# Modulation products of a two-layer diffusion backbone: in pairs on TensorE, one more sixth summed on VectorE, and a norm's first high parts on VectorE

## The chip, the cores and the metric

The kernel runs on one core of a Trainium2 chip. The metric is the device time of one execution in microseconds (us); the comparison is between medians of several executions of the kernel before and of the changed kernel.

## The reference, cut to what matters

Two layers of a hybrid diffusion backbone act on 256 latent tokens and 256 context tokens of width 1024. A conditioning vector gives, for each layer, a modulation of six parts (shift, scale and gate for the mixer and for the feed-forward part), for the latent and the context stream:

```python
mod = jax.nn.silu(c) @ w_mod[l] + b_mod[l]
mod_c = jax.nn.silu(c_ctx) @ w_mod[l] + b_mod[l]
sh1, sc1, g1, sh2, sc2, g2 = jnp.split(mod[:, None, :], 6, axis=-1)
h = rmsnorm(x, g_pre_mix[l]) * (1 + sc1) + sh1
y, y_ctx = token_mixer(h, hc, lp, row, col, ctx_out)
x = x + g1 * rmsnorm(y, g_post_mix[l])
h2 = rmsnorm(x, g_pre_ffn[l]) * (1 + sc2) + sh2
x = x + g2 * rmsnorm(conv_ffn(h2, ...), g_post_ffn[l])
```

The mixer has four branches (latent attention, a bidirectional mLSTM, window attention, a Fourier mix), each gated by a product of `h` with a 1024x1024 matrix and summed. The reference is in float32.

## The kernel before, in words

Activations stand feature by feature: eight tiles of 128 features by the tokens. Each float32 factor of a large product is split into a high and a low part, and each product is three matmuls: high by high (line L236), and the two cross terms (L237, L238). The weights come by DMA on SyncE's queue into `st`; ScalarE casts the high part `wh` (L216), VectorE subtracts it to get the low part `wl` (L217).

The order of TensorE's instructions is written out by hand: wherever a stage would leave TensorE waiting for another engine, `fill(us)` takes matmuls from independent work of another stage (most of them gate products of `merge`). VectorE's, ScalarE's and GpSimd's orders are made by the scheduler, save inside `in_order()`. Each engine's instructions stand in a fixed order once the program is built.

The modulation is done by `mod_rounds` (L608 to L671). A round is one of the six parts: eight k tiles of `w_mod`, each [128, 4x256], which arrive by DMA (L625) on GpSimd's queue in the first layer (rounds 2 to 4) and on SyncE's elsewhere. A step is one k tile: four 32-column matmuls of line L653, whose records come in eights. `between(n)` takes n steps from `queue`, and `fill` takes them where they are fillers. A round that is listed in `vector` is summed on VectorE instead: two sums over the k tiles, one for each stream, by L640 for the first tile and L642 for the other seven, and at the end eight matmuls with a column of ones (L648, 16 records). A round ends with a transpose `kr` (L656) and an addition of the bias (L664, L667). In the first layer round 3 was summed on VectorE; rounds 2 and 4 were taken by `pause` (L896), `mla` (L960) and by the merge, one step at a time.

The places of the first layer that the steps speak of: the latent attention's softmax (`nbias` L831, exponential on ScalarE L835, reciprocal L840, scaled `pp` L841, transposed on TensorE at L847); the mLSTM's gates in `mlstm_gates` (`gcum` L1055, `gb` L1056, a product on TensorE at L1059, its copy `t` L1061, three running scans L1066 to L1068, and eight small products on TensorE at L1072); and the last head's normalisation in `mlstm` (`mden` L1216, `mab`, `mrec`, sums into `u` at L1226, then a product on TensorE at L806).

In the last layer's `channel` the norm ahead of the feed-forward part is written in order: the mean square's transposed root `rs` (L457), then for each feature tile m the product with `rs` (`t`, L405), the scaled high part `hh` on ScalarE (L408), the same number in float32 on VectorE for the first two tiles (L410) and on ScalarE for the rest (L412), and the low part `hl` by subtraction on VectorE (L414). TensorE's first products of the feed-forward part read `hh` (L236) and `hl` (L237).

Of the kernel before, what the change touches and what calls it, by code (L numbers as in the profile page):

```python
# [14 lines left out]
AF = mybir.ActivationFunctionType  # L15
ALU = mybir.AluOpType
# [6 lines left out]
T = CTX + SEQ  # L23
# [134 lines left out]
class Net:  # L158
# [237 lines left out]
        for _ in self.modulate_steps(h, m, segs, r, Am, Bm, vector):  # L396
            pass

    def modulate_steps(self, h, m, segs, r, Am, Bm, vector=False):

        nc = self.nc
        oc = self.span(segs)
        hi, lo = h[m]
        t = self.t2([T])
        nc.vector.tensor_tensor(t[:, oc], self.xcols(m, oc), r[:, oc], op=ALU.mult)  # L405
        for cs, b in segs:
            a, s = Am[:, m, b:b + 1], Bm[:, m, b:b + 1]
            nc.scalar.activation(hi[:, cs], t[:, cs], AF.Identity, scale=a, bias=s)  # L408
            if vector:
                nc.vector.tensor_scalar(t[:, cs], t[:, cs], a, s, op0=ALU.mult, op1=ALU.add)  # L410
            else:
                nc.scalar.activation(t[:, cs], t[:, cs], AF.Identity, scale=a, bias=s)  # L412
        yield
        nc.vector.tensor_tensor(lo[:, oc], t[:, oc], hi.bitcast(F32)[:, oc], op=ALU.subtract)  # L414
# [193 lines left out]
    def mod_rounds(self, l, rounds, queue, vector=(), parts=1):  # L608

        nc = self.nc
        if rounds[0] == 0:
            self.mods[l] = self.cp.tile([128, 48, 2], F32, tag=f"mod{l}", name=f"mod{l}")
        mods = self.mods[l]
        todo = [(r, q, k) for r in rounds for q in range(parts) for k in range(0, KT, parts)]
        loaded = []
        n = 256 // parts

        def load():  # L620
            if todo:
                r, q, k = todo.pop(0)
                st = self.u([parts, 4, n])
                src = self.A["wmod"][l, r, k] if parts == 1 else self.A["wmod0"][r, q, k // 2]
                queue.dma_start(out=st.rearrange("p a g n -> p (a g n)"), in_=src)  # L625
                for i in range(parts):
                    loaded.append((r, q, k + i, st[:, i]))

        def steps():
            b = self.vec[l][:, V_BMOD:V_BMOD + 48].unsqueeze(2).to_broadcast([128, 48, 2])  # L630
            while loaded or todo:
                if not loaded:
                    load()
                r, q, k, st = loaded.pop(0)
                if r in vector:
                    if k == 0:
                        sums = [self.u([4, 256]) for _ in range(2 if l < L - 1 or r < 2 else 1)]
                    for i, t in enumerate(sums):
                        if k == 0:
                            nc.vector.tensor_scalar(t, st, self.cs[:, k, i:i + 1], None, op0=ALU.mult)  # L640
                        else:
                            nc.vector.scalar_tensor_tensor(t, st, self.cs[:, k, i:i + 1], t, op0=ALU.mult, op1=ALU.add)  # L642
                    if k == KT - 1:
                        yield 1
                        ps = self.pa([256])
                        for i, t in enumerate(sums):
                            for g in range(4):
                                nc.tensor.matmul(ps[32 * g:32 * g + 32], self.col[:, i], t[:, g], start=i == 0, stop=i == len(sums) - 1)  # L648
                else:
                    if k == 0:  # L650
                        ps = self.pa([n])
                    for g in range(4):
                        nc.tensor.matmul(ps[32 * g:32 * g + 32], self.cs[:, k], st[:, g], start=k == 0, stop=k == KT - 1)  # L653
                if k == KT - 1:
                    tr = self.t2([n], tag="kr")
                    nc.vector.transpose(tr, ps)  # L656
                    src = tr.rearrange("p (t c) -> p t c", c=32)[:, :, 0:2]
                    if r < 2:
                        a = 2 // parts
                        src = src.rearrange("p (a s m) t -> p a s m t", a=a, s=2)  # L660
                        for i in range(2):
                            o = slice(8 * i + 4 * r + 2 * q, 8 * i + 4 * r + 2 * q + 2 * a)
                            fold = lambda t: t.rearrange("p (a m) t -> p a m t", a=a)
                            nc.vector.tensor_tensor(fold(mods[:, o]), src[:, :, i], fold(b[:, o]), op=ALU.add)  # L664
                    else:
                        o = slice(8 * r, 8 * r + 8)
                        nc.vector.tensor_tensor(mods[:, o], src, b[:, o], op=ALU.add)  # L667
                if k % parts == parts - 1:
                    load()
                yield 1200  # L670

        return steps(), load

# [219 lines left out]

    def pause(self, i, c0):
        self.fill(1.5 + i)
        self.between(((4, 0), (0, 5))[c0 > 0][i])  # L896

    def mla(self, l, h, c0):

        nc = self.nc  # L900
# [56 lines left out]
            self.rows = rows  # L957
            self.rope(q[rows, CTX:], ps[rows, CTX:], self.kc(C_MCOS, 256, rows), self.kc(C_MSIN, 256, rows), perm)
        self.fill(1)
        self.between((2, 3)[c0 > 0])  # L960
        rs = [slice(0, 96), slice(0, 128)]
        y = self.newy()
        room = (1.2, 1.2)
# [547 lines left out]
    def run(self):  # L1511
        nc = self.nc
# [9 lines left out]
        h = self.new_h()  # L1522
        A = None
        self.wtm = []
        mod, load = self.mod_rounds(0, (0, 1), nc.sync, parts=2)
# [3 lines left out]
        for q in range(4):  # L1529
# [6 lines left out]
            A, B = self.gain(0, 1, V_GPRE, True, "A1", ms, A), self.shift(0, 0)  # L1536
# [2 lines left out]
            if q == 0:  # L1539
                self.tm_start(h, NT)  # L1540
        self.start2()
        mod, load = self.mod_rounds(0, (2, 3, 4), nc.gpsimd, (3,))
        self.queue = [mod]
        for l in range(L):
            last = l == L - 1
            c0 = CTX if last else 0
# [16 lines left out]
    def channel(self, l, al, c0, load):  # L1563
# [11 lines left out]
        for seg in segs:  # L1575
            open_steps = []
            with self.in_order() if last else nullcontext():
                if last:
                    self.post_end([seg], True, [lambda f=f, m=m: f(m, [seg]) for m in range(2) for f in (self.scale, self.add)])
                    self.fill(1.5)  # L1580
                for m in range(KT):
                    if seg is not segs[-1] and m == 4:
                        self.post_end(segs[1:], True)
                    if m >= (2 if last else 4) or not last and seg is segs[-1]:
                        self.residual(m, [seg])
                    open_steps.append(self.modulate_steps(h, m, [seg], self.rx, A, B, last and m < 2))
                    next(open_steps[-1])
                    while len(open_steps) > (1 if last and m < KT - 1 else 0):
                        next(open_steps.pop(0), None)
                    if seg is segs[-1] and not last:  # L1590
                        self.spill(m, c0, c0)
        next(self.ws)
# [48 lines left out]
```

## Time and profile before

| what | value |
|---|---|
| median of 3 runs | 1441.56 us (1439.45 to 1442.52) |
| profiled execution | 1440.69 us |
| its span | 1438.5 us |
| mean granted TensorE clock | 0.989 |
| busy share of the span, PE / DVE / ACT / POOL | 97% / 66% / 46% / 2% |
| chain that ended last, by engine | PE 77%, DVE 7%, ACT 1%, DMA 1% |

PE is TensorE's matmuls, PEld its weight loads, DVE VectorE, ACT ScalarE, POOL GpSimd, SP SyncE. The span is that of the profiled execution, which is one run of its own; 2.2 us of its time lie outside the span. An engine's busy share is a mean over stages that have different limits, so the rows further down are taken stage by stage.

### The profile page before, as it was taken

To read this page: it belongs to the slowest core of one execution; us is meant where nothing else is said; L and a number is where in the kernel's file an instruction comes from. 1 tells how busy PE (TensorE), PEld (TensorE's weight loads), DVE (VectorE), ACT (ScalarE), POOL (GpSimd) and SP (SyncE) were. 2 spreads that over 40 slices of the span, in tenths; PEclk is the share of its full clock that TensorE was granted. 3 is DMA by queue.
4 is the path that set the end of the run, shared out by engine and by line. 5 is a ranking of instruction groups with operands and counts; after the bars stand their busy time and mean duration, and the time that the engine had idled before them with its cause. 6 is when DMAs were issued, how large, how long until landed. Compare 5 with 4: busy or idle time off the path is not lost.

```text
span 1438.5 us, 21680 instructions
## 1 busy us (share of the span) xinstructions
PE 1389.9 (97%) x8413; PEld 1165.3 (81%) x8413; DVE 949.4 (66%) x1942; ACT 659.5 (46%) x1144; POOL 33.3 (2%) x65
## 2 busy tenths in 40 slices
PE   6999999999999999999999999899999999899997
PEld 4977777777778888878888888687989898799996
DVE  5458686646644788743554658958676877766666
ACT  3446444224432655333322336656453655455553
POOL 0000000100000000000000000100000000000000
PEclk9999999999999999999999999999999999899999
DMA  9523233452122634443335432653333457255663
GB/s 373 209 71 103 89 118 103 147 163 87 59 74 88 219 125 172 172 133 103 130 115 180 160 93 79 222 199 103 106 115 118 135 189 248 85 180 176 186 184 114
DMA packets 57446, 205.86 MB, mean 143 GB/s; under 512 B 6528, under 2 KB 6912, under 8 KB 57216
## 3 DMA queue, kind: packets, MB, share of 16 engines
q1 hardware_dynamic: 50400, 179.32, 37.9%
q0 software_dynamic: 6944, 25.17, 5.1%
q8 instruction: 66, 1.08, 0.3%
q14 instruction: 36, 0.29, 0.1%
HBM read 200.27 MB, written 4.19 MB: 142 GB/s over the span
## 4 chain that ended last, share of the span: by engine, by line
PE 77%; DVE 7%; ACT 1%; issue 1%; DMA 1%; DVEq 0%; ACTq 0%
PE pg L236 16%; PE pg L237 15%; PE pg L238 15%; PE pa L238 6%; PE pa L237 6%; PE pa L236 6%; PE pa L794 2%; PE pa L824 1%; PE pa L1461 1%; DVE wl L217 1%; PE pa L1462 1%; PE pa L1460 1%; PE pa L863 1%; PE pa L847 1%; PE pa L653 1%
## 5 line engine op out<-in xcount | busy, mean ns | idle before, releaser
L217 DVE TENSOR_TENSOR wl<-st,wh 128x1024 fp32r<-128x1024 f32 (+2 forms) x260 | 313.5, 1210 | 224.8 <-ACT wh L216 223.5
L216 ACT CAST wh<-st 128x1024 fp32r<-128x1024 f32 (+2 forms) x260 | 268.5, 1039 | 358.2 <-PE pg L237 192.7
L236 PE MATMUL pg<-hh,wh 128*128 128x512 f32 (+1 forms) x1136 | 404.3, 356 | 0.7 <-DVE tg L1273 0.7
L238 PE MATMUL pg<-hh,wl 128*128 128x512 f32 (+1 forms) x1136 | 385.4, 339 | 1.5 <-DVE wl L217 1.5
L237 PE MATMUL pg<-hl,wh 128*128 128x512 f32 (+1 forms) x1136 | 384.8, 339 | 0.0
L236 PEld LDWEIGHTS pg<-hh,wh 128*128 128x128 f32 x1136 | 217.0, 191 | 30.9 <-issue 5.9
L238 PEld LDWEIGHTS pg<-hh,wl 128*128 128x128 f32 x1136 | 216.8, 191 | 25.9 <-DVE wl L217 2.3
L237 PEld LDWEIGHTS pg<-hl,wh 128*128 128x128 f32 x1136 | 217.2, 191 | 23.1 <-issue 3.1
L236 PE MATMUL pa<-hh,wh 128*128 128x256 f32 (+1 forms) x376 | 125.9, 335 | 1.4 <-ACT hh L292 1.4
L237 PE MATMUL pa<-hl,wh 128*128 128x256 f32 (+1 forms) x376 | 126.0, 335 | 0.1
L238 PE MATMUL pa<-hh,wl 128*128 128x256 f32 (+1 forms) x376 | 125.9, 335 | 0.0
L236 PE MATMUL pg<-u,wh 128*128 128x512 f32 (+1 forms) x255 | 93.0, 365 | 0.8 <-ACT tg L1264 0.8
L238 PE MATMUL pg<-u,wl 128*128 128x512 f32 (+1 forms) x255 | 88.6, 347 | 0.0
L237 PE MATMUL pg<-u,wh 128*128 128x512 f32 (+1 forms) x255 | 88.4, 347 | 0.0
L236 PEld LDWEIGHTS pa<-hh,wh 128*128 128x128 f32 x376 | 71.2, 189 | 9.5 <-ACT hh L292 1.6
L237 PEld LDWEIGHTS pa<-hl,wh 128*128 128x128 f32 x376 | 71.2, 189 | 8.6 <-DVE hl L293 0.7
L238 PEld LDWEIGHTS pa<-hh,wl 128*128 128x128 f32 x376 | 71.2, 189 | 7.1
L642 DVE SCALAR_TENSOR_TENSOR u<-u,cs,u 128x1024 f32<-128x1024 f32 x49 | 61.6, 1278 | 1.6 <-DMA u<-wmod 1.6
L835 ACT ACTIVATE pp<-pa,nbias 128x512 f32<-128x512 f32 (+1 forms) x48 | 29.5, 615 | 68.1 <-DVE nbias L833 37.2
L236 PEld LDWEIGHTS pg<-u,wh 128*128 128x128 f32 x255 | 48.2, 189 | 12.8 <-issue 5.9
L237 PEld LDWEIGHTS pg<-u,wh 128*128 128x128 f32 x255 | 48.2, 189 | 6.4 <-issue 0.7
L408 ACT ACTIVATE hh<-t,mod,A 128x256 fp32r<-128x256 f32 x56 | 32.1, 595 | 46.5 <-DVE t L405 29.3
(315 smaller groups left out, 2172.4 us busy)
## 6 DMA issues: line engine op xcount, KB each, us to landing
st<-wup SPq DMA_DIRECT2D x88, 512.0 KB, 3.6
u<-wmod SPq DMA_DIRECT2D x64, 512.0 KB, 5.5
st<-wgate SPq DMA_DIRECT2D x64, 512.0 KB, 3.6
u<-wmod POOLq DMA_DIRECT2D x32, 512.0 KB, 4.8
st<-win SPq DMA_DIRECT2D x26, 512.0 KB, 3.8
st<-wdt SPq DMA_DIRECT2D x22, 512.0 KB, 3.5
st<-wbr SPq DMA_DIRECT2D x16, 512.0 KB, 3.6
st<-wout SPq DMA_DIRECT2D x16, 512.0 KB, 3.7
```

The source lines that it names most:

```text
L216: nc.scalar.copy(hi[:, :cols], st[:, :cols])
L217: nc.vector.tensor_tensor(lo[:, :cols], st[:, :cols], hi.bitcast(F32)[:, :cols], op=ALU.subtract)
L236: mm(out, ah, bh, start=i == 0, stop=False)
L237: mm(out, ah, bl, start=False, stop=False)
L238: mm(out, al, bh, start=False, stop=i == n - 1)
L408: nc.scalar.activation(hi[:, cs], t[:, cs], AF.Identity, scale=a, bias=s)
L642: nc.vector.scalar_tensor_tensor(t, st, self.cs[:, k, i:i + 1], t, op0=ALU.mult, op1=ALU.add)
L653: nc.tensor.matmul(ps[32 * g:32 * g + 32], self.cs[:, k], st[:, g], start=k == 0, stop=k == KT - 1)
L794: ins = self.nc.tensor.matmul(O[:, j], lhs[i], rhs[i], start=i == 0, stop=i == n - 1)
L824: nc.tensor.matmul(S[:, :n], q, k, start=i == 0, stop=i == len(ops) - 1 and not m)
L835: nc.scalar.activation(P[:, :n], S[:, :n], AF.Exp, bias=nb, scale=scale, accum_out=den)
L847: nc.tensor.transpose(S[:, j * 128:j * 128 + 128], P[:, j * 128:j * 128 + 128], self.ident)
```

## The change

In `mod_rounds`, rounds on TensorE keep two k tiles loaded and are taken two steps at a time (a step now ends after an odd k, with twice the credit); the counts of `between` in `pause` and `mla` are halved to match. In the first layer round 4, the fifth sixth, is summed on VectorE too. In the last layer's norm the high parts of the first two tiles are made on VectorE and their float32 twins on ScalarE, and the `fill(1.5)` stands after the fourth tile instead of ahead of the first.

```diff
@@ modulate_steps
-    def modulate_steps(self, h, m, segs, r, Am, Bm, vector=False):
+    def modulate_steps(self, h, m, segs, r, Am, Bm, vector=False, first=False):
...
         nc.vector.tensor_tensor(t[:, oc], self.xcols(m, oc), r[:, oc], op=ALU.mult)
+        if first:
+            (cs, b), = segs
+            a, s = Am[:, m, b:b + 1], Bm[:, m, b:b + 1]
+            e = self.t2([T])
+            nc.vector.tensor_scalar(hi[:, cs], t[:, cs], a, s, op0=ALU.mult, op1=ALU.add)
+            nc.scalar.activation(e[:, cs], t[:, cs], AF.Identity, scale=a, bias=s)
+            t = e
+            segs = ()
         for cs, b in segs:
...
@@ mod_rounds, steps
             while loaded or todo:
-                if not loaded:
+                while todo and len(loaded) < (1 if todo[0][0] in vector else 2):
                     load()
                 r, q, k, st = loaded.pop(0)
...
                 if k % parts == parts - 1:
                     load()
-                yield 1200
+                if parts > 1 or r in vector:
+                    yield 1200
+                elif k % 2:
+                    yield 2400
@@ pause
-        self.between(((4, 0), (0, 5))[c0 > 0][i])
+        self.between(((2, 0), (0, 3))[c0 > 0][i])
@@ mla
-        self.between((2, 3)[c0 > 0])
+        self.between((1, 1)[c0 > 0])
@@ run
-        mod, load = self.mod_rounds(0, (2, 3, 4), nc.gpsimd, (3,))
+        mod, load = self.mod_rounds(0, (2, 3, 4), nc.gpsimd, (3, 4))
@@ channel
                     self.post_end([seg], True, [lambda f=f, m=m: f(m, [seg]) for m in range(2) for f in (self.scale, self.add)])
-                    self.fill(1.5)
                 for m in range(KT):
...
-                    open_steps.append(self.modulate_steps(h, m, [seg], self.rx, A, B, last and m < 2))
+                    open_steps.append(self.modulate_steps(h, m, [seg], self.rx, A, B, first=last and m < 2))
                     next(open_steps[-1])
                     while len(open_steps) > (1 if last and m < KT - 1 else 0):
                         next(open_steps.pop(0), None)
+                    if last and m == 3:
+                        self.fill(1.5)
```

Lines of the changed kernel stand 8 further down from `modulate_steps` on, and 11 or 12 further down behind `mod_rounds`: L640, L642 and L648 become L648, L650 and L656; L1061 and L1066 to L1068 become L1072 and L1077 to L1079.

**VectorE's order at the mLSTM's gates, first layer.** Before:

```order
L642 SCALAR_TENSOR_TENSOR u_1658<-u_1941,cs,u_1658 128x1024
L1055 COPY gcum_1950<-pa_1927 128x2x4x4
L1056 TENSOR_TENSOR gb_1951<-gt_535,gcum_1950 128x32
L217 TENSOR_TENSOR wl_2045<-st_2042,wh_2044 128x1024
L1271 SCALAR_TENSOR_TENSOR acc_530<-tg_1937,pg_1943 128x512
L1061 COPY t_415_1959<-pa_1954 8x512
L1066 SCALAR_TENSOR_TENSOR u_1987<-t_415_1959 8x512
L1067 SCALAR_TENSOR_TENSOR u_1987<-t_415_1959 8x256
L1068 SCALAR_TENSOR_TENSOR u_1987<-t_415_1959,u_1987 8x256
```

And in the changed kernel:

```order
L650 SCALAR_TENSOR_TENSOR u_1560<-u_1869,cs,u_1560 128x1024
L1066 COPY gcum_1956<-pa_1933 128x2x4x4
L650 SCALAR_TENSOR_TENSOR u_1561<-u_1869,cs,u_1561 128x1024
L1067 TENSOR_TENSOR gb_1957<-gt_535,gcum_1956 128x32
L1282 SCALAR_TENSOR_TENSOR acc_530<-tg_1943,pg_1949 128x512
L217 TENSOR_TENSOR wl_2051<-st_2048,wh_2050 128x1024
L1072 COPY t_417_1965<-pa_1960 8x512
L650 SCALAR_TENSOR_TENSOR u_1560<-u_1947,cs,u_1560 128x1024
L1077 SCALAR_TENSOR_TENSOR u_1993<-t_417_1965 8x512
L1078 SCALAR_TENSOR_TENSOR u_1993<-t_417_1965 8x256
L650 SCALAR_TENSOR_TENSOR u_1561<-u_1947,cs,u_1561 128x1024
L1079 SCALAR_TENSOR_TENSOR u_1993<-t_417_1965,u_1993 8x256
```

Round 3 now begins earlier on VectorE, and three of its passes (L650) stand between `gcum` and the last scan, where none stood. TensorE's instructions between its product of `gb` and the eight products that read the scans are the same eighteen matmuls in both kernels.

**VectorE's order at the last head's normalisation, first layer.** Before:

```order
L1216 COPY mden_2692<-pa_2674 128x4
L1217 SCALAR_TENSOR_TENSOR mab_2693<-mden_2692 128x4
L1218 TENSOR_TENSOR mab_2693<-mab_2693,gE_2019 128x4
L1219 RECIPROCAL mrec_2685<-mab_2693 128x4
L1225 TENSOR_TENSOR pp_2698<-pa_2674,mrec_2685 128x256
L1226 TENSOR_TENSOR u_2021<-u_2021,pp_2698 128x4x64
```

And in the changed kernel:

```order
L1227 COPY mden_2700<-pa_2682 128x4
L1229 TENSOR_TENSOR mab_2695<-mab_2695,gE_2025 128x4
L650 SCALAR_TENSOR_TENSOR u_2639<-u_2643,cs,u_2639 128x1024
L1230 RECIPROCAL mrec_2681<-mab_2695 128x4
L1228 SCALAR_TENSOR_TENSOR mab_2701<-mden_2700 128x4
L650 SCALAR_TENSOR_TENSOR u_2640<-u_2643,cs,u_2640 128x1024
L1229 TENSOR_TENSOR mab_2701<-mab_2701,gE_2025 128x4
L1235 TENSOR_TENSOR u_2027<-pa_2670,mrec_2681 128x4x64
L1230 RECIPROCAL mrec_2693<-mab_2701 128x4
L1236 TENSOR_TENSOR pp_2706<-pa_2682,mrec_2693 128x256
L1237 TENSOR_TENSOR u_2027<-u_2027,pp_2706 128x4x64
```

Two passes of round 4 stand between the copy of the second denominator and the sum `u` that TensorE reads. TensorE has nine matmuls in between in both kernels.

**VectorE's order at the last layer's norm.** Before:

```order
L457 STREAM_TRANSPOSE rs_11585<-n_2323_11722 128x256
L656 STREAM_TRANSPOSE kr_11752<-pa_11654 128x256
L667 TENSOR_TENSOR mod_529<-kr_11752,vec_82 128x16
L405 TENSOR_TENSOR t_2325_11755<-u_11278,rs_11585 128x256
L685 TENSOR_TENSOR G_11820<-mod_529,vec_82 128x16
L410 TENSOR_SCALAR t_2325_11755<-t_2325_11755,A_11647,mod_529 128x256
L405 TENSOR_TENSOR t_2326_11759<-u_11278,rs_11585 128x256
L410 TENSOR_SCALAR t_2326_11759<-t_2326_11759,A_11647,mod_529 128x256
L414 TENSOR_TENSOR hl_11631<-t_2325_11755,hh_11630 128x256
```

And in the changed kernel:

```order
L465 STREAM_TRANSPOSE rs_11579<-n_2325_11720 128x256
L405 TENSOR_TENSOR t_2326_11738<-u_11272,rs_11579 128x256
L410 TENSOR_SCALAR hh_11624<-t_2326_11738,A_11641,mod_529 128x256
L405 TENSOR_TENSOR t_2328_11743<-u_11272,rs_11579 128x256
L410 TENSOR_SCALAR hh_11626<-t_2328_11743,A_11641,mod_529 128x256
L422 TENSOR_TENSOR hl_11625<-t_2327_11740,hh_11624 128x256
```

The transpose `kr`, the sum `mod` and the gain `G` have moved behind the third low part, and `hh` of the first two tiles is written here.

## Rows read from the trace of the kernel before

**Rows 1.** The page's busy time by engine over the span.

```profile
PE 1389.9 (97%) x8413; PEld 1165.3 (81%) x8413; DVE 949.4 (66%) x1942; ACT 659.5 (46%) x1144; POOL 33.3 (2%) x65
```

**Rows 2.** Busy us by stretch: PE, PEld, DVE, ACT, POOL (instructions); PEclk, DMA share, GB/s.

```profile
200.00:366.00 166.00, 166.00 (x858) 127.13 (x858) 107.81 (x245) 63.68 (x139) 7.37 (x14) 1.00 0.35 111
```

**Rows 3.** Timeline of PE, lone modulation steps: start, us, line, operands, [idle before].

```profile
286.07 0.40 PE L237 MATMUL pg<-hl,wh 128*128 128x512 f32 x1
286.31 0.40 PE L238 MATMUL pg<-hh,wl 128*128 128x512 f32 x1
286.64 0.64 PE L653 MATMUL pa<-u,cs 128*32 128x256 f32 x8
...
287.55 0.39 PE L237 MATMUL pg<-u,wh 128*128 128x512 f32 x1
...
363.30 0.64 PE L653 MATMUL pa<-u,cs 128*32 128x256 f32 x8
```

**Rows 4.** Timeline of PE, the column batch that ends round 3.

```profile
273.63 1.07 PE L648 MATMUL pa<-u,col 128*32 128x256 f32 x16
```

**Rows 5.** Timeline of DVE, the latent attention's last softmax.

```profile
187.37 1.28 DVE L642 SCALAR_TENSOR_TENSOR u<-u,cs,u 128x1024 f32<-128x1024 f32 x1 [0.68 <-DMA u<-wmod]
188.57 0.48 DVE L841 TENSOR_SCALAR pp<-pp,rec 128x512 f32<-128x512 f32 x1
188.97 0.68 DVE L852 COPY pp<-pa 128x512 f32<-128x512 f32 x1
```

**Rows 6.** Timeline of PE, the transpose that reads the last pp.

```profile
190.13 0.60 PE L847 MATMUL pa<-k,pp 128*128 128x128 f32 x4
```

**Rows 7.** Timeline of DVE, the mLSTM's gates.

```profile
200.06 0.19 DVE L1055 COPY gcum<-pa 128x32 f32<-128x32 f32 x1 [2.36 <-PE pa L1049]
...
204.77 0.74 DVE L1068 TENSOR_TENSOR_SCAN u<-t,u 8x256 f32<-8x256 f32 x1
```

**Rows 8.** Timeline of PE, the eight products that read the scans.

```profile
205.99 0.66 PE L1072 MATMUL pa<-k,u 8*128 8x8 f32 x8
```

**Rows 9.** Timeline of DVE, the last head's normalisation.

```profile
282.81 0.16 DVE L1216 COPY mden<-pa 128x4 f32<-128x4 f32 x1 [1.00 <-PE pa L794]
...
284.07 0.42 DVE L1226 TENSOR_TENSOR u<-u,pp 128x256 f32<-128x256 f32 x1
```

**Rows 10.** Timeline of PE, the product that reads u.

```profile
284.71 0.38 PE L806 MATMUL pa<-k,u 128*128 128x128 f32 x2
```

**Rows 11.** Timeline of PE, three waits in the second layer.

```profile
1001.01 1.09 PE L847 MATMUL pa<-k,pp 128*128 128x128 f32 x4 [2.71 <-DVE pp L841]
...
1051.25 0.36 PE L1157 MATMUL pa<-u,sel 96*128 96x256 f32 x1 [1.79 <-DVE u L1085]
...
1200.48 0.38 PE L236 MATMUL pa<-hh,wh 128*128 128x256 f32 x1 [1.35 <-ACT hh L292]
```

**Rows 12.** Busy us by stretch behind those waits, columns as in rows 2.

```profile
1001.00:1004.00 3.00, 2.99 (x14) 3.00 (x15) 3.00 (x6) 1.79 (x4) 0.00 (x0) 0.50 0.00 0
1051.00:1055.00 4.00, 3.75 (x20) 3.78 (x21) 2.64 (x5) 3.35 (x10) 0.00 (x0) 0.60 0.39 152
1201.00:1204.00 3.00, 3.00 (x25) 3.00 (x26) 1.51 (x2) 2.12 (x4) 0.00 (x0) 1.00 0.94 345
1237.00:1243.00 6.00, 5.96 (x28) 5.96 (x29) 5.73 (x16) 3.60 (x6) 0.00 (x0) 0.50 0.02 4
```

**Rows 13.** Timeline of PE, a modulation step at the second layer's start.

```profile
529.11 0.64 PE L653 MATMUL pa<-u,cs 128*32 128x256 f32 x8 [0.72 <-DMA u<-wmod]
```

**Rows 14.** Timeline of DVE, the last layer's norm.

```profile
1232.84 0.45 DVE L457 STREAM_TRANSPOSE rs<-n 128x256 f32<-128x256 f32 x1
...
1236.57 0.42 DVE L414 TENSOR_TENSOR hl<-t,hh 128x256 fp32r<-128x256 f32 x1
```

**Rows 15.** Timeline of PE, the first products behind that norm.

```profile
1234.85 0.58 PE L236 MATMUL pg<-hh,u 128*128 128x256 f32 x1 [3.28 <-ACT hh L408]
1237.04 0.58 PE L237 MATMUL pg<-hl,u 128*128 128x256 f32 x1 [1.61 <-DVE hl L414]
```

## The prediction

> **What bounds the kernel now.** I read the page's busy time first, then busy time by stretch, then timelines around each place that the change touches, and last the order of VectorE's instructions in both kernels. TensorE (PE) is busy 97% of the span and VectorE (DVE) 66% [rows 1]. From 200 to 366 us, where most of the first layer's modulation rounds lie, PE is busy 166.00 of 166 us and DVE 107.81 [rows 2]: work taken off PE there comes off the end one for one, as long as DVE delivers in time. That last condition is what the whole forecast hangs on, since a mean of 65% says nothing of how late the next thing is that PE waits for.
>
> All terms are made against the profiled execution, 1440.69 us (span 1438.5, 2.2 us around it); it lies 0.87 us under the median of the three runs, 1441.56. About 0.2%, 2.9 us, is what a measurement of this kernel can tell from no change.
>
> **Round 4 leaves PE.** In [rows 3] one product starts 0.24 us behind another (286.07 to 286.31), so two take 0.48. With a lone modulation step in between, the second product behind 286.31 starts at 287.55, 1.24 us on: a lone step costs 0.76 us, of which 0.64 is its own busy time. Round 4 has eight of them, the first at 286.64 and the last at 363.30; they go: 8 x 0.76 = **-6.1 us**. In their place comes one more column batch, of 16 records and 1.07 us [rows 4]. Sixteen records are 0.43 us more than eight, so it costs 0.76 + 0.43 = **+1.2 us**. On DVE come two shorter first passes and fourteen of 1.28 us [rows 5], under 16 x 1.28 = 20.5 us. DVE has 58 us idle in that stretch [rows 2], so by capacity they cost nothing. The DMAs stay on GpSimd's queue, eight in place of eight; the four loads of x behind them now wait for DVE's sums rather than PE's steps, and their data are needed only for the residual behind the whole mixer. In the second layer two more loads stand ahead of GpSimd's copies of the keys, which come much later; SyncE's order is unchanged.
>
> **Where DVE's passes now stand.** DVE runs its instructions in their written order, and the order shown with the change puts passes inside three chains that PE waits for. A pass takes 1.28 us by itself and about 1.2 from start to start (187.37 to 188.57 in [rows 5]).
>
> - Attention's last softmax. Before, one pass stood ahead of the last `pp`, which ended at 188.57 + 0.48 = 189.05; PE read it at 190.13 without a wait [rows 5, 6], so 1.08 us were spare. Now two passes of the third tile and the 0.6 us copy that stood behind `pp` are ahead of it: 1.2 + 0.6 - 1.08 = +0.7 us.
> - The mLSTM's gates. `gcum` waits for PE (2.36 us idle before 200.06), so nothing can be done earlier, and the last scan ends at 205.51 [rows 7]. PE starts its eight small products at 205.99 and ends them at 206.65 [rows 8]; the last two read that scan, so some 0.9 us are spare. Three passes now stand between: 3 x 1.2 - 0.9 = **+2.7 us** of PE waiting.
> - The last head. `mden` waits for PE at 282.81, `u` ends at 284.49 [rows 9], PE reads it at 284.71 [rows 10]: 0.2 us spare. Two passes and some reordered short rows stand between: 2 x 1.2 - 0.2 + 0.2 = **+2.4 us**.
>
> Together +5.8 us. The bounds: nothing, if the passes find the queue empty earlier than I read it (-5.8), and +8, if a tile's landing holds a pass at the queue's head, as [rows 5] shows once with 0.68 us. I take the middle, since order and durations are known.
>
> **What the waits do to PE's clock.** After waits of 2.71 and 1.79 us [rows 11] the granted clock reads 0.50 and 0.60 in the next 3 to 4 us, the lower of the two levels, 1.2 of 2.4 GHz; after a wait of 1.35 it reads 1.00 [rows 12]. The two new waits, 2.4 to 2.7 us, lie between the first two, so I expect some 3 us at half rate behind each, which loses half of that: 2 x 1.5 = **+3.0 us**. Bounds: 0, as behind 1.35; and 2 x 3 = 6, as in the 6 us at 0.50 behind the norm of the last layer. I take the nearer rows. The Trainium skill, page "TensorE: Matmul & The Clock Gate", section "Part 1: The HAM clock gate (the "warmup" mystery)", has it that the slow clock is the default state and that activity lifts it, so by that rule a wait costs more than its length. By it the term stays at its +3.0; the trace agrees behind 2.71 us (0.50) and not behind 1.35 us (1.00), and if the new waits are like the latter the sum is 3.0 us less.
>
> **The pairs.** A second step right behind a first costs 0.43 instead of 0.76. In the first layer two lone steps of round 2 become one pair: -0.33 us. In the second layer's two openings the lone step at the end of each is also drawn in (-0.76 each), but the last pair must wait for its second tile. Before, PE waited 0.72 us for a tile's landing and then took 0.64 for its step [rows 13]; a pair at the end waits for one tile more, 0.72 + 0.64 = 1.4 us later. I take **0** for both openings together, with -1.3 and +1.8 as ends. The other rounds go from five and three steps at one place to six and two, which is nothing.
>
> **The last norm.** Before, `rs` starts at 1232.84, `hh` comes from ScalarE and PE starts at 1234.85; `hl` starts at 1236.57 and PE goes on at 1237.04 [rows 14, 15]. Now DVE does after `rs` five rows of 0.34 to 0.45 us (`t`, `hh`, `t`, `hh`, `hl`), with ScalarE's twin beside them: `hl` ends near 1232.84 + 0.45 + 0.45 + 0.4 + 0.4 + 0.4 + 0.4 = 1235.3, and PE goes on 1.7 us earlier. `kr`, `mod` and `G`, three short rows, come later, where PE runs behind DVE. Behind that everything is products, so the gain stays: **-1.7 us**; ends -0.6 (half the clock lasts to the same point) and -3 (it ends sooner).
>
> **The sum**: -6.1 + 1.2 + 5.8 + 3.0 - 0.33 + 0 - 1.7 = +1.87. That is 1442.6 for a run like the profiled one, and 1443.4 beside the median: no change that can be told, on the slow side.
>
> **Rivals.**
> *DVE hides its passes (faster).* For it: 58 idle us [rows 2]. Against it: the chains above wait for PE, so that idle time can't be used ahead of them. Without the waits and their clock the sum is 1.87 - 5.8 - 3.0 = -6.9: 1434.6 beside the median. With one of the two large waits it is about -6.9 + 2.5 + 1.5 = -2.9, 1438.7. The Trainium skill, page "PSUM — Partial Sum Buffer", section "Engine vs sequencer instructions", calls VectorE's queue strict FIFO; by that rule this rival falls wherever the order puts a pass inside a chain, and the wait at 1051.25 for DVE's `u` [rows 11] agrees that PE waits for such chains.
> *Half rate lasts longer (slower).* At the last norm the clock stays at 0.50 for 6 us [rows 12] after 3.28 and 1.61 us of waiting [rows 15]. If the two new waits, each followed by shorter ones, do the same, each loses 3 instead of 1.5: 1.87 + 3.0 = +4.9, 1446.4. It decides from about 4 us of half rate each (1.87 + 2 x 0.5 = +2.9). Against it: two of the three rows show about 3.
> *Pairs wait for landings (slower).* With the upper end of the two openings the sum is 1.87 + 1.8 = +3.7, 1445.2; for it the 0.72 us wait [rows 13], against it that loads are issued as buffers fall free, thus partly earlier.
> That the change doesn't do what it says is shut out by the order, which shows the passes moved.
>
> **How the numbers follow.** The forecast has 0.41; the first rival 0.26 (0.24 of it beyond 0.2%); the second 0.21, the third 0.12. Faster by over 0.2% (under 1438.7) 0.24; within 0.2% 0.43, the forecast and the inner edges of the others; slower (over 1444.4) 0.33. The range reaches from 1434.5, the first rival's time, to 1447.5, past the second's.
>
> **What would show it.** In the changed kernel: no L661 rows between 286 and 364 us, two L656 batches in the first layer; PE waits of 2 to 3 us for DVE at the scans (near 206) and at `u` (near 285), with PEclk near 0.5 behind them; PE's first L237 behind the last norm 2.4 to 2.6 us after `rs`. No such waits, and the first rival holds. A time under 1438.7 or over 1446.4 makes the forecast wrong.

## The result, and the profile after

The changed kernel takes 1447.87 us (median of 6 runs, 1447.58 to 1453.96), the kernel before 1439.78 us (median of 6 runs, 1436.26 to 1442.52, the three of the table above among them). The ratio of the runs is 1.0073, 95% interval 1.0057 to 1.0088: 0.7% or, by that ratio, 10.5 us **slower** (the two medians as they stand are 8.1 us apart). The prediction, 1443.4 in a range up to 1447.5, had the sign of its sum right and its size too small. The profiled execution took 1447.79 us, span 1446.0.

The page of the changed kernel, busy time; the line answers to [rows 1]:

```profile
PE 1387.3 (96%) x8365; PEld 1165.0 (81%) x8365; DVE 965.1 (67%) x1958; ACT 659.2 (46%) x1144; POOL 34.2 (2%) x65
```

PE has less work, as meant, and the kernel is longer: PE waits more. The timeline of PE has these waits over one microsecond between 100 and 380 us; in the kernel before there is none over 0.7 us in that stretch:

```profile
132.43 0.41 PE L858 MATMUL pa<-k,pp 128*128 128x128 f32 x2 [1.05 <-DVE pp L852]
...
137.85 0.33 PE L874 MATMUL pa<-pp,u 128*64 128x128 f32 x2 [2.13 <-ACT pp L861]
...
190.91 0.33 PE L858 MATMUL pa<-k,pp 128*128 128x128 f32 x1 [1.14 <-DVE nbias L842]
...
197.85 0.44 PE L858 MATMUL pa<-k,pp 128*128 128x128 f32 x1 [3.50 <-DVE pp L852]
...
218.14 0.37 PE L1083 MATMUL pa<-k,u 8*128 8x8 f32 x2 [1.55 <-DVE u L1079]
...
300.75 0.33 PE L817 MATMUL pa<-k,u 128*128 128x128 f32 x1 [2.02 <-DVE u L1237]
```

Set the same PE instruction of both traces side by side, and the changed kernel's lag grows and shrinks like this (times are those of before):

| stretch, us | what happens in the changed kernel | lag changes by, us |
|---|---|---|
| to 31 | first loads of the program, the same code in both | +0.8 |
| 130 to 134 | waits 1.05 and 2.13 (0.52 before) | +3.0 |
| 134 to 186 | a pair for two lone steps, small rest | -0.8 |
| 186 to 190 | waits 1.14 and 3.50 | +4.7 |
| 190 to 206.2 | half rate behind, small waits | +2.3 |
| 206.3 | wait 1.55 | +1.7 |
| 206.4 to 211 | half rate behind | +1.6 |
| 211 to 284 | small rest (round 3's column batch comes earlier) | +0.4 |
| 284.8 | wait 2.02 | +2.25 |
| 287 to 376 | eight lone steps gone, a column batch added | -4.7 |
| together | | +11.2 |

From 376 to 960 us the lag grows by 0.9. From there to the end it shrinks by 5.6. Of that 0.7 falls at the last norm; the rest can't be put down to the change, since each trace of the experiments below, with its parts or without, is 2.6 us or more shorter there than this one execution of before, whose waits and half rates stand in [rows 11, 12]. The ratio over all runs is what counts.

**Why PE waits at 197.85.** The timeline of VectorE (DVE) around attention's last softmax, which answers to [rows 5]:

```profile
187.85 0.75 DVE L648 TENSOR_SCALAR u<-u,cs 128x1024 f32<-128x1024 f32 x1
188.52 0.15 DVE L851 RECIPROCAL rec<-den 128x1 f32<-128x1 f32 x1
188.59 0.67 DVE L840 TENSOR_REDUCE nm<-pa 128x1 f32<-128x512 f32 x1
189.18 1.27 DVE L650 SCALAR_TENSOR_TENSOR u<-u,cs,u 128x1024 f32<-128x1024 f32 x1
190.37 0.48 DVE L852 TENSOR_SCALAR pp<-pp,rec 128x512 f32<-128x512 f32 x1
190.77 0.14 DVE L842 TENSOR_SCALAR nbias<-nm 128x1 f32<-128x1 f32 x1
194.16 2.48 DVE L650 SCALAR_TENSOR_TENSOR u<-u,cs,u 128x1024 f32<-128x1024 f32 x2 [3.25 <-DMA u<-wmod]
196.56 0.16 DVE L851 RECIPROCAL rec<-den 128x1 f32<-128x1 f32 x1
196.63 0.67 DVE L863 COPY pp<-pa 128x512 f32<-128x512 f32 x1
197.22 0.48 DVE L852 TENSOR_SCALAR pp<-pp,rec 128x512 f32<-128x512 f32 x1
```

From 190.91 to 194.16 VectorE stands still with the third tile's pass at its head, which waits for the tile to land; `rec`, the copy and the last `pp` stand behind it, and PE reads `pp` at 197.85. The tiles' loads, in the timeline of POOL:

```profile
179.09 0.96 POOL L633 DMA_DIRECT2D u<-wmod  x1 [30.70 <-issue]
187.87 0.85 POOL L633 DMA_DIRECT2D u<-wmod  x1 [7.82 <-ACT pp L846]
188.90 0.53 POOL L633 DMA_DIRECT2D u<-wmod  x1 [0.18 <-DVE rec L851]
190.75 0.53 POOL L633 DMA_DIRECT2D u<-wmod  x1 [1.32 <-DVE u L650]
```

The third tile is the load issued at 187.87. In the built program it takes the buffer of a half of the queries and waits for attention's last score, which reads it and starts on PE at 186.27. (The row names ScalarE's exponential, which ended shortly before the issue; the load has no wait for it in the program.) It lands at 194.14, 6.27 us after its issue: SyncE's own queue issues a load of weights at almost the same moment, and two more tiles follow:

```profile
187.96 0.33 SPq L205 DMA_DIRECT2D st<-win  x1
```

In the kernel before, the third tile waits for the second tile's passes only, is issued at 183.46 (1.05 us behind the start of the last score, here 1.60) and lands 3.88 us later, as SyncE's load comes 2.1 us behind it; the rest of that wait is the 0.68 us of [rows 5]. The Trainium skill, page "DMA: Bandwidth & Descriptors", section "Issuing engines are not separate DMA queues", says that loads of different engines share the same 16 DMA engines and interleave; 3.88 against 6.27 us for the same 512 KB agrees.

**132 to 138 us.** The timeline of ScalarE (ACT), first of the changed kernel, then of the kernel before:

```profile
134.42 0.62 ACT L308 CAST u<-t 64x512 fp32r<-64x512 f32 x1 [0.76 <-DVE t L1117]
...
136.33 0.62 ACT L309 CAST u<-t 64x512 fp32r<-64x512 f32 x1
136.97 0.47 ACT L846 ACTIVATE pp<-pa,nbias 128x256 f32<-128x256 f32 x1
```

```profile
133.21 0.46 ACT L835 ACTIVATE pp<-pa,nbias 128x256 f32<-128x256 f32 x1
133.56 0.19 ACT L835 ACTIVATION_READ_ACCUMULATOR pp<-pa,nbias 128x1 f32 x1
133.65 0.36 ACT L850 COPY pp<-pa 128x256 f32<-128x256 f32 x1
134.06 0.62 ACT L308 CAST u<-t 64x512 fp32r<-64x512 f32 x1
```

A softmax's exponential, which stood ahead of four casts, now stands behind them: 2.5 us, and PE's wait of 2.13. The wait of 1.05 ahead of it is of the same kind: a weight's cast `wh` (L216, at 127.45 on ScalarE) and its low part `wl` (L217, at 128.51 on VectorE) now stand ahead of a softmax's exponential and its scaled `pp`, and stood behind them before (129.60 and 130.69). PE's order is the same up to here; only where the other engines' rows are placed differs. Why the scheduler places them so is not shown.

**The gates**, which answer to [rows 7]. Three passes stand between `gcum` and the last scan, as the order has it. The first (209.46) ends ahead of `gb` and costs PE 0.17 us there; the other two stand between the copy that feeds the scans and the last scan:

```profile
213.27 1.26 DVE L650 SCALAR_TENSOR_TENSOR u<-u,cs,u 128x1024 f32<-128x1024 f32 x1
214.46 1.21 DVE L1077 TENSOR_TENSOR_SCAN u<-t 8x512 f32<-8x512 f32 x1
215.59 0.65 DVE L1078 TENSOR_TENSOR_SCAN u<-t 8x256 f32<-8x256 f32 x1
216.18 1.25 DVE L650 SCALAR_TENSOR_TENSOR u<-u,cs,u 128x1024 f32<-128x1024 f32 x1
217.35 0.73 DVE L1079 TENSOR_TENSOR_SCAN u<-t,u 8x256 f32<-8x256 f32 x1
```

**The clock** behind the waits of 3.50, 1.55 and 2.02 us, columns as in [rows 2]:

```profile
198.00:201.00 3.00, 3.00 (x10) 2.52 (x10) 2.77 (x4) 0.58 (x1) 0.53 (x1) 0.50 0.60 175
...
218.00:221.00 3.00, 2.86 (x8) 2.35 (x9) 2.94 (x7) 2.81 (x5) 0.00 (x0) 0.52 0.00 0
...
300.75:304.00 3.25, 3.25 (x17) 2.67 (x18) 1.55 (x4) 1.86 (x4) 0.00 (x0) 0.95 0.15 61
```

In this execution the clock reads 0.95 wherever others read 1.00 (the last section says more), so behind the 2.02 us it did not fall. That is this one execution's. The changed kernel with lone steps in the second layer, among the experiments below, has the same first layer, and there the same wait is followed by 3.4 us at 0.50 (a row of PE's timeline and a stretch behind it):

```profile
299.21 0.33 PE L817 MATMUL pa<-k,u 128*128 128x128 f32 x1 [2.02 <-DVE u L1237]
...
300.02:303.44 3.42, 3.42 (x12) 2.63 (x10) 1.44 (x3) 2.17 (x4) 0.00 (x0) 0.50 0.03 11
```

In the same way the wait of 2.13 us near 138 stands in six of the traces; in three the clock reads 0.50 behind it, and in three, the changed kernel's among them, it does not fall. So half rate behind a given wait is in part a matter of the single execution.

**The last norm**, timelines of DVE and of PE, which answer to [rows 14, 15]: from `rs` to PE's second product it is 2.52 us (4.20 before), and the first product waits for VectorE's `hh` instead of ScalarE's. Measured from PE's last step ahead of the norm, 0.7 of these 1.68 us are left, since `rs` itself comes 1.0 us later behind that step than before.

```profile
1240.84 0.45 DVE L465 STREAM_TRANSPOSE rs<-n 128x256 f32<-128x256 f32 x1
...
1242.89 0.42 DVE L422 TENSOR_TENSOR hl<-t,hh 128x256 fp32r<-128x256 f32 x1
```

```profile
1242.24 0.57 PE L236 MATMUL pg<-hh,u 128*128 128x256 f32 x1 [3.63 <-DVE hh L410]
1243.36 0.58 PE L237 MATMUL pg<-hl,u 128*128 128x256 f32 x1 [0.55 <-DVE hl L422]
```

### The profile page after: what moved, and what is told of

It reads as the page before. It is cut to its first block, busy times and chain, and to the rows that moved or that the text cites. A ratio compares the mean times of both kernels' runs of the same rounds, so it can differ in the third digit from the quotient of the medians.

```text
span 1446.0 us, 21589 instructions
## 1 busy us (share of the span) xinstructions
PE 1387.3 (96%) x8365; PEld 1165.0 (81%) x8365; DVE 965.1 (67%) x1958; ACT 659.2 (46%) x1144; POOL 34.2 (2%) x65
## 3 DMA queue, kind: packets, MB, share of 16 engines
q8 instruction: 66, 1.08, 0.3%
## 4 chain that ended last, share of the span: by engine, by line
PE 53%; DVE 8%; ACT 2%; issue 2%; DMA 2%; DVEq 0%; ACTq 0%
PE pg L236 9%; PE pg L237 9%; PE pg L238 9%; PE pa L237 6%; PE pa L238 6%; PE pa L236 6%; DVE wl L217 1%; PE pa L1472 1%; PE pa L1473 1%; PE pa L1471 1%; ACT wh L216 1%; PE pa L805 1%; DMA st<-wup 1%; DMA st<-wgate 1%; PE pa L835 1%
## 5 line engine op out<-in xcount | busy, mean ns | idle before, releaser
L217 DVE TENSOR_TENSOR wl<-st,wh 128x1024 fp32r<-128x1024 f32 (+2 forms) x260 | 313.8, 1211 | 214.8 <-ACT wh L216 213.6
L216 ACT CAST wh<-st 128x1024 fp32r<-128x1024 f32 (+2 forms) x260 | 268.7, 1040 | 357.0 <-PE pg L237 188.8
L650 DVE SCALAR_TENSOR_TENSOR u<-u,cs,u 128x1024 f32<-128x1024 f32 x63 | 78.9, 1276 | 4.2 <-DMA u<-wmod 4.1
L238 PEld LDWEIGHTS pg<-u,wl 128*128 128x128 f32 x255 | 48.1, 189 | 6.6
```

Of the source, the lines that this page charges most:

```text
L216: nc.scalar.copy(hi[:, :cols], st[:, :cols])
L217: nc.vector.tensor_tensor(lo[:, :cols], st[:, :cols], hi.bitcast(F32)[:, :cols], op=ALU.subtract)
L238: mm(out, al, bh, start=False, stop=i == n - 1)
```

## The experiments

**Theory.** The sixteen added passes are harmless; the pairs do the harm. They come with a loop that holds two tiles ahead where one was held, and they start round 3 one pull earlier. The loop asks for two tiles on TensorE's rounds alone, but each step still ends with a load, so the second tile that round 2 held is carried on through VectorE's rounds 3 and 4. **Rivals:** the added passes are the harm; the norm is; the second layer's openings wait for landings. Every run below is in five rounds against the kernel before; ratios are to it, with their 95% intervals. All differences are under 2%; "faster" and "slower" mean that the interval leaves out 1.

### One part alone

The kernel before with round 4 on VectorE:

```diff
-        mod, load = self.mod_rounds(0, (2, 3, 4), nc.gpsimd, (3,))
+        mod, load = self.mod_rounds(0, (2, 3, 4), nc.gpsimd, (3, 4))
```

> The kernel before with round 4 summed on VectorE and nothing else. Theory (the pairs did the harm, by starting round 3 one pull earlier): VectorE's rows up to the last head stand as before, so the 3.50 us wait near 198 and the 1.55 us wait near 218 are absent; round 4 saves 6.1 us of steps, costs 1.2 us of column batch and about 2.2 us at the last head: 2.7 us faster than before, ratio near 0.998, and 4.9 us faster (0.9966) if the last head does not wait. Rival (VectorE's sixteen added passes did the harm): 5 us or more slower than before, ratio 1.003 or more, with waits of PE for VectorE behind 200 us.

Measured: 1434.31 us, ratio 0.9974 (0.9960 to 0.9988). **Faster.** No wait over 0.6 us from 100 to 380 us. The seven lone steps between PE's instructions at 287 and 364 us take the lag to before from -1.75 to -6.85, 0.73 us each, where 0.76 was predicted; the column batch then gives back 1.1. At the last head the first passes of round 4 stand behind `u`, not ahead of it:

```profile
282.99 0.42 DVE L1226 TENSOR_TENSOR u<-u,pp 128x256 f32<-128x256 f32 x1
...
285.62 1.41 DVE L640 TENSOR_SCALAR u<-u,cs 128x1024 f32<-128x1024 f32 x2
```

So the rival of the added passes falls: they cost nothing where they begin behind that chain.

The kernel before with the pairs, their loads and their pulls:

```diff
-                if not loaded:
+                while todo and len(loaded) < (1 if todo[0][0] in vector else 2):
                     load()
...
-                yield 1200
+                if parts > 1 or r in vector:
+                    yield 1200
+                elif k % 2:
+                    yield 2400
...
-        self.between(((4, 0), (0, 5))[c0 > 0][i])
+        self.between(((2, 0), (0, 3))[c0 > 0][i])
...
-        self.between((2, 3)[c0 > 0])
+        self.between((1, 1)[c0 > 0])
```

> The kernel before with the steps in pairs and the changed numbers of pulls, round 4 still on TensorE, the old norm. Theory: the waits near 132 to 138 (3.0 us), 191 and 198 (4.6 us) and 218 (1.5 us) are there as in the changed kernel, with the half rate behind them (2.8 us), less 0.33 us for each of five pairs in the first layer: about 10 us slower, ratio 1.007. Rival (the added passes did the harm): between 1.6 us faster and 1.8 us slower than before, ratio 0.999 to 1.001, no such waits.

Measured: 1448.84 us, ratio 1.0069 (1.0045 to 1.0093). **Slower**, as much as the whole change, though the change has two more parts that help. The timeline of its PE:

```profile
138.14 0.33 PE L866 MATMUL pa<-pp,u 128*64 128x128 f32 x2 [2.13 <-ACT pp L853]
...
199.45 0.30 PE L850 MATMUL pa<-k,pp 128*128 128x128 f32 x1 [3.40 <-DVE pp L844]
...
219.80 0.28 PE L1075 MATMUL pa<-k,u 8*128 8x8 f32 x2 [1.55 <-DVE u L1071]
```

Three of the changed kernel's waits are there to 0.1 us without one added pass. The 2 us at the last head are not: in the changed kernel they come from round 4's passes inside that chain, so they need both the pairs and round 4 on VectorE.

The kernel before with the last norm's new rows and the moved fill:

```diff
+        if first:
...
-                    self.fill(1.5)
...
-                    open_steps.append(self.modulate_steps(h, m, [seg], self.rx, A, B, last and m < 2))
+                    open_steps.append(self.modulate_steps(h, m, [seg], self.rx, A, B, first=last and m < 2))
...
+                    if last and m == 3:
+                        self.fill(1.5)
```

> The kernel before with the last norm's first two high parts on VectorE and the fill moved behind the fourth tile, nothing else. Both theories: 0.7 us (what the traces of the two kernels differ by over this stretch) to 1.7 us (as predicted) faster than before, ratio 0.999 to 0.9995; PE starts its first products behind the norm at most 2.6 us after rs. A ratio over 1.001 would make the norm part of the loss.

Measured: 1434.84 us, ratio 0.9989 (0.9972 to 1.0006). The size is as expected, and the interval just reaches no change. From PE's last step ahead of the norm to its second product its trace gains 1.4 us on before (0.7 in the changed kernel), and `rs` to that product is 2.52 us here too.

Multiplied, the three ratios give 1.0032 and not the change's 1.0073, 5.9 us less. The last head's 2.25 us are in none of the three; the rest, some 3.7 us, is within what the intervals leave open.

### Two tiles ahead, or round 3 a pull early?

The pairs bring both. The changed kernel with the last pair of round 2 in two pulls, so that round 3 begins where it did:

```diff
-                elif k % 2:
+                elif k % 2 or l == 0 and k > 5:
                     yield 2400
```

> The changed kernel with the last pair of round 2 taken in two pulls again, so that round 3 begins at the same merge as in the kernel before. Theory: one pair of VectorE's passes fewer stands ahead of attention's last softmax and of the gates, so the 3.50 us wait near 198 goes, with its half rate (1.2 us), and about 1.3 us of the gates' wait: 5 to 8 us faster than the changed kernel, 1440 to 1443 us; the waits near 132 to 138 stay. Rival (the sixteen added passes did the harm): within 2 us of the changed kernel, ratio to before about 1.007.

Measured: 1437.87 us, ratio 1.0000 (0.9985 to 1.0015): 10 us faster than the changed kernel, more than expected. But the wait did not go:

```profile
194.51 0.30 PE L858 MATMUL pa<-k,pp 128*128 128x128 f32 x1 [2.65 <-DVE pp L852]
```

Of the 3.50 us 0.85 went, with the gates' and the last head's waits and the half rate. In the built program the third tile's load waits for attention's last score here too. An early round 3 makes things worse and is not the root.

The changed kernel, pulls as they are, with one tile ahead of VectorE's rounds:

```diff
-                if k % parts == parts - 1:
+                if k % parts == parts - 1 and not (loaded and todo and todo[0][0] in vector):
                     load()
```

> The changed kernel, pairs and pulls as they are, but with one tile loaded ahead of VectorE's rounds instead of two. Theory (a tile held ahead keeps a buffer, so the third tile's load of round 3 takes the buffer that attention's last score frees and lands 6 us later at the head of VectorE's queue): the third tile's load is issued some 5 us earlier against the last score, the 3.50 us wait near 198 shrinks to under 1 us and the gates' 1.55 us goes; the waits near 132 to 138 (3.2 us) stay, since round 2 still loads two ahead: about 0.9963 + 3.2/1440 = 0.9985 of before (0.998 to 0.9995), some 12 us faster than the changed kernel. Rival (that round 3 begins one pull earlier is the harm, whatever is loaded when): the waits stay, 1.004 or more of before.

Measured: 1433.15 us, ratio 0.9962 (0.9949 to 0.9976), 1.1% under the changed kernel. The waits of 3.50 and 1.55 us are gone and those near 132 to 138 are there (1.08 and 2.14 us), as the theory has it; the time is better than the range expected. Its timelines of POOL and of DVE:

```profile
178.55 0.53 POOL L633 DMA_DIRECT2D u<-wmod  x1 [31.73 <-DVE u L648]
185.29 1.69 POOL L633 DMA_DIRECT2D u<-wmod  x3 [6.21 <-DVE u L650]
```

```profile
188.35 0.16 DVE L851 RECIPROCAL rec<-den 128x1 f32<-128x1 f32 x1 [0.37 <-ACT pp L846]
189.18 2.48 DVE L650 SCALAR_TENSOR_TENSOR u<-u,cs,u 128x1024 f32<-128x1024 f32 x2 [0.66 <-DMA u<-wmod]
191.58 0.48 DVE L852 TENSOR_SCALAR pp<-pp,rec 128x512 f32<-128x512 f32 x1
```

Two passes stand ahead of the last `pp` here too, and cost PE nothing, since the third tile waits 0.66 us and not 3.25. The theory's "5 us earlier" was wrong, though: the load is issued 0.94 us behind the start of the last score instead of 1.60, only 0.7 us earlier; another 2.4 us are its landing, 3.86 us instead of 6.27, as SyncE's `win` load now follows 2.1 us later. How the loss splits between the late issue and the shared transfer was not tried by itself. Nor does the edit leave the two later places alone: with it a single pass stands between `gcum` and the last scan, and none inside the last head's chain, where the 2.02 us wait is gone as well. So there it was VectorE's order that changed, not a landing.

The changed kernel with one tile ahead in the first layer throughout, round 2 too:

```diff
-                while todo and len(loaded) < (1 if todo[0][0] in vector else 2):
+                while todo and len(loaded) < (1 if todo[0][0] in vector or l == 0 else 2):
                     load()
```

> The changed kernel with its pairs and pulls, but in the first layer each step loads one tile ahead, as before, also in round 2. Theory (the second tile held ahead is the whole harm, near 132 to 138 too, where ScalarE's exponential stands behind four casts): no wait over 1 us in the first layer; 0.995 to 0.998 of before. Rival (the early round 3 is the harm): a wait of 2 us or more near 198, 1.002 or more of before.

Measured: 1436.07 us, ratio 0.9983 (0.9970 to 0.9995), just above the range expected. Now ScalarE's exponential is back ahead of its casts, and neither the waits near 132 to 138 nor the one near 198 are there. But the theory's "no wait over 1 us" failed, at the pair itself:

```profile
145.38 0.42 PE L661 MATMUL pa<-u,cs 128*32 128x256 f32 x4 [4.04 <-DMA u<-wmod]
```

The pair's second tile was loaded only behind the pair's first step, at 141.66. That is the prediction's third rival, in the first layer: a pair needs its second tile ahead, and the tile ahead needs a buffer.

### Without the pairs, and with them in the second layer alone

Both parts that help, lone steps, loads and pulls of before (the kernel with the norm alone, edited as the first one):

```diff
-        mod, load = self.mod_rounds(0, (2, 3, 4), nc.gpsimd, (3,))
+        mod, load = self.mod_rounds(0, (2, 3, 4), nc.gpsimd, (3, 4))
```

> The changed kernel without its pairs: lone steps, loads and numbers of pulls as before; round 4 on VectorE and the new norm stay. Theory (all of the loss comes with the pairs): the two parts add up, 0.9974 x 0.9989 = 0.9963 of before, 5.3 us faster. Rival (the parts hinder each other): 0.998 or more.

Measured: 1431.28 us, ratio 0.9949 (0.9934 to 0.9965): the parts add up, and a little more.

The same with pairs, their loads and their pulls in the second layer only (written as edits to the changed kernel):

```diff
-                while todo and len(loaded) < (1 if todo[0][0] in vector else 2):
+                while todo and len(loaded) < (1 if todo[0][0] in vector or l == 0 else 2):
                     load()
...
-                if parts > 1 or r in vector:
+                if parts > 1 or r in vector or l == 0:
                     yield 1200
...
-        self.between(((2, 0), (0, 3))[c0 > 0][i])
+        self.between(((4, 0), (0, 3))[c0 > 0][i])
...
-        self.between((1, 1)[c0 > 0])
+        self.between((2, 1)[c0 > 0])
```

> As the kernel without pairs, but with the pairs, their loads and their numbers of pulls in the second layer alone. Theory (the harm lies in the first layer): within 2 us of the kernel without pairs, 0.995 to 0.9977 of before. Rival (part of the loss is waits for landings in the second layer's openings): 2 us or more slower than it, 0.998 or more of before.

Measured: 1431.38 us, ratio 0.9945 (0.9928 to 0.9962): the same as without pairs, 0.1 us from it. Both kernels beat before by 0.5% and the changed kernel by more than 1.2%.

In the traces, though, kernels with pairs in the second layer are 5 to 9 us shorter than before from 960 us on, those without 2.6 to 4.2. To see whether that is the pairs, the opposite edit, lone steps in the second layer, was made to the changed kernel

```diff
-                while todo and len(loaded) < (1 if todo[0][0] in vector else 2):
+                while todo and len(loaded) < (1 if todo[0][0] in vector or l else 2):
                     load()
...
-                if parts > 1 or r in vector:
+                if parts > 1 or r in vector or l:
                     yield 1200
...
-        self.between(((2, 0), (0, 3))[c0 > 0][i])
+        self.between(((2, 0), (0, 5))[c0 > 0][i])
...
-        self.between((1, 1)[c0 > 0])
+        self.between((1, 3)[c0 > 0])
```

> The changed kernel with lone steps, their loads and their numbers of pulls in the second layer, everything in the first layer as changed. Theory (the harm lies in the first layer alone, the second layer's pairs are neutral): within 2 us of the changed kernel, 1.006 to 1.0087 of before. Rival (the second layer's pairs gain 3 us, as the traces of the kernels with them hint behind 960 us): 1.0085 to 1.0105 of before.

Measured: 1447.53 us, ratio 1.0065 (1.0051 to 1.0078), the changed kernel's time; and to the kernel with one tile ahead of VectorE's rounds, with the same four edits and, in the first layer, its own:

```diff
-                if k % parts == parts - 1:
+                if k % parts == parts - 1 and not (l == 0 and loaded and todo and todo[0][0] in vector):
                     load()
```

> The kernel with one tile ahead of VectorE's rounds, with lone steps, their loads and their numbers of pulls in the second layer. Theory (second layer's pairs neutral): 0.995 to 0.9976 of before, as with them (0.9962). Rival (they gain 3 us): 0.9975 to 0.999.

Measured: 1433.98 us, ratio 0.9966 (0.9954 to 0.9978), against 0.9962 with them. Three times over, pairs in the second layer neither help nor harm (0.9949 and 0.9945, 1.0065 and 1.0073, 0.9966 and 0.9962). The hint was single executions: the traced ones with these pairs lie up to 3.1 us under their kernels' medians (one 0.2 above), those without up to 7.2 above (one 0.6 under).

PE's waits over 0.25 us from 100 to 380 us, added up from each trace, against the ratio:

| kernel | tiles ahead in round 2 / VectorE's rounds | round 3 begins | waits, us | ratio |
|---|---|---|---|---|
| before | 1 / 1 | as before | 1.7 | 1 |
| no pairs, new norm, round 4 on VectorE | 1 / 1 | as before | 1.7 | 0.9949 |
| one ahead of VectorE's rounds | 2 / 1 | a pull early | 4.3 | 0.9962 |
| one ahead throughout | 1 / 1 | a pull early | 5.8 | 0.9983 |
| last pair in two pulls | 2 / 2 | as before | 7.4 | 1.0000 |
| the change | 2 / 2 | a pull early | 12.0 | 1.0073 |

The last five have the norm and round 4 alike, and their ratios rise in the order of their waits. So do the other three kernels that have both: 1.7 us and 0.9945 with pairs in the second layer alone, 4.4 and 0.9966, 11.9 and 1.0065 with lone steps there.

## Why the prediction was wrong, by its own steps

- **Round 4 leaves PE**, -6.1 + 1.2: right. Alone it measured 0.73 us a step and 1.1 us for the batch, and 0.26% in all.
- **Attention's last softmax**, +0.7: this step failed. It counted DVE's rows and their durations and took the middle "since order and durations are known". What decides there is when the third tile's load can be issued and lands, which no row of DVE's order tells. VectorE waited 3.25 us for that landing, and the stretch measured +4.7, with +2.3 of half rate and small waits behind it. The case stood among the bounds ("a tile's landing holds a pass at the queue's head"), with its 0.68 us from [rows 5], but the change's own new load condition was not followed to the ring of 16 buffers, where one more tile is held and the next load takes a buffer that attention frees last. The prediction counted round 4's loads ("eight in place of eight"); the one that hurt is round 3's, whose number did not change and whose moment did.
- **Not in the sum at all**, and so put at nothing: the order of ScalarE's and VectorE's rows at 132 to 138 us, +3.0. I looked at DVE's order where the change moves passes, and not at the other engines where it moves none.
- **The gates**, +2.7: right in kind, measured +1.7. Three passes stand there, but only two between the copy and the last scan, and 2 x 1.2 - 0.9 = 1.5 is the wait of 1.55. **The last head**, +2.4: measured +2.25 with a wait of 2.02.
- **Half rate**, +3.0 as 2 x 1.5: of the two waits named, it follows the gates' (0.52) and not the last head's; it also follows the softmax's 3.50 us, which was not named. 1.2 us are lost up to 200.4 us behind the softmax and 1.6 behind the gates. The size is right, but where it falls is partly luck, as the same waits in other traces show. By the Trainium skill's rule in "TensorE: Matmul & The Clock Gate", section "Part 1", that activity lifts a slow default, the term stood. This trace agrees behind 3.50 and 1.55 us, and not behind 2.13 and 2.02.
- **The pairs**, -0.33 and 0: in the trace the first layer's pair gains 0.2 us (lag 3.70 at 140 us, 3.48 at 154), and the second layer's 0 was measured three times. The price lay in what keeps them fed.
- **The last norm**, -1.7: from `rs` on it is 1.68, as worked out; that `rs` comes later leaves 0.7 in the trace of the change and 1.4 in the kernel with the norm alone, within the ends of -0.6 and -3.
- **The rivals.** "DVE hides its passes" holds of the change without its pairs, at 0.9949. "Half rate lasts longer" came nearest with its 1446.4, but not by its mechanism: the clock reads half for 3.4 us behind each of the two waits, under the 4 from which that rival decides. "Pairs wait for landings" was put in the second layer and happens in the first, to VectorE's passes.

With the terms at their measured sizes the sum is 1.87 + 4.0 (softmax) + 3.0 (rows at 132 to 138 us) - 1.0 (gates) - 0.15 (last head) + 0.9 (half rate and small waits, 2.3 + 1.6 instead of 3.0) + 1.0 (norm) = +9.6; the ratio has 10.5. A more careful reading would have walked POOL's queue: for each load, whose buffer it takes and what frees that, and then which pass stands on it at VectorE's head.

## What to carry to other kernels

When a change loads one tile further ahead, find out whose buffer the next load takes, and what releases it last: in a full ring the cost can appear at a load some tiles later, here the third, and not at the one that was brought forward. A row that waits for a landing at the head of an in-order engine holds up every short row behind it, so its price is the landing, not its own duration. Where a kernel's order is planned, compare all engines' orders at the places where PE waits for them, also where the change adds nothing.

## What the runs showed of the hardware that was not expected

- The length of a wait does not alone decide the clock: behind the same wait of 2.13 us it fell to 0.50 in three traces and not in three others, and behind the same 2.02 us it read 0.95 in one execution and 0.50 in another.
- The third tile's 512 KB landed in 3.79 to 3.99 us in the eight kernels where SyncE's next load came 2.1 us behind it, and in 6.16 to 6.35 us in the four where that came within 0.15 us of it. These four are also the ones that hold two tiles ahead in VectorE's rounds.
- In this one execution of the changed kernel the granted clock reads 0.95 where others read 1.00 (1447.79 us with a mean of 0.94, 1449.22 with 0.988), at the same spacing of products, 0.23 us: that reading cost no time.
